# One pass instead of two for the second half's operands, and stores and loads two at a time, in the FFN of a one-core encoder block

## The chip, the cores and the metric

The kernel runs on one core of a Trainium2 chip. The metric is the device time of one execution in microseconds (us); lower is better. The time before is the median of three runs.

## What is computed

The kernel computes one layer of an encoder for 2048 tokens of width 1024: three gated token mixers, then a feed-forward network with a causal convolution of width 3, then a last norm. The change touches only the feed-forward part and the last norm:

```python
def conv_ffn(h, w_in, conv_w, conv_b, w_out):
    u, gv = jnp.split(h @ w_in, 2, axis=-1)
    T = u.shape[1]
    up = jnp.pad(u, ((0, 0), (CONV_W - 1, 0), (0, 0)))
    uc = conv_w[0] * up[:, 0:T]
    for j in range(1, CONV_W):
        uc = uc + conv_w[j] * up[:, j:j + T]
    uc = uc + conv_b
    return (jax.nn.gelu(uc, approximate=False) * gv) @ w_out
...
        x = x + conv_ffn(rms_norm(x, norm_ffn_g[l]), w_ffn_in[l], ffn_conv_w[l],
                         ffn_conv_b[l], w_ffn_out[l])
    return rms_norm(x, norm_final_g)
```

D_FF is 2816, so `w_ffn_in` is 1024 by 5632 and `w_ffn_out` 2816 by 1024. Everything is float32; each float32 product is made of three matmuls on a high and a low part (hi*hi, hi*lo, lo*hi).

## The kernel before

Tokens lie on the free axis, channels on the 128 partitions. The feed-forward part (`ffn`) works on two halves of 1024 tokens (`hf` 0 and 1), each of two tiles of 512 tokens (`t` 0 and 1). The 2816 inner channels are 22 blocks `f` of 128.

**First product.** `in_block(f)` makes the 128 channels of u and of the gate for both token tiles with seven products instead of eight (a Strassen-like scheme). Each product is 12 matmuls of 128x128 by 128x512 and needs one weight piece `wsp` of 512 KB, and for each a right operand `B[m][k]`, m from 1 to 7 and k from 0 to 3, 128x512 in hi and lo. The order of the products is 1, 2, 6, 5, 3, 7, 4. In the second half the weight pieces are read from a cache in DRAM (`wc_w_ffn_in`).

**The operands.** `ffn_prep(hf, B)` makes them from `x2d` (the residual stream in DRAM). `quarter(k, t)` loads a block of 128 channels by 512 tokens (256 KB) into one of eight staging places and norms it with one VectorE (DVE) instruction, a scalar_tensor_tensor on line 725 (L725). `put` writes a block as hi (a copy on ScalarE, ACT, L729) and lo (a subtract on DVE, L730); `minus` is a subtract on DVE (L733). Block pair k has the four quarters b11, b12, b22 and b21. B[1] and B[2] are b11 and b21 as they are and lie in the tile `hA`; the other five are differences. A first loop norms b11 and b21 of each k and puts them into `hA`; a second loop norms all four quarters of each k (so b11 and b21 again) and makes the other five. The generator gives way eight times, four per loop.

**Second product.** `out_group(f0)` multiplies two blocks f with `w_ffn_out`: 16 output tiles (8 channel blocks d by 2 token tiles), each 6 matmuls into a PSUM bank (L924 to L926) and one DVE add into the accumulator `acc` in SBUF (L928). Its weights are four pieces per group (`w_out`), each loaded as 256 KB into `wraw`, cast to hi on ACT (L138) and subtracted to lo on GpSimd (POOL, L141). `wraw` has three buffers, and staging places of `quarter` are `wraw` buffers too.

**Where the halves meet.** At the end of the first half stand two groups, `out_group(NF - 4)` (banks `mx` and `ch`) and `out_group(NF - 2)` (banks `mm`), 32 tiles in all. After every third tile (`SK = 3`) `step()` takes one step of `ffn_prep(1)`. These groups I call A and B.

**The start of the second half.** During f = 0 and 1 the first half's `acc` is squared and summed; `finish_scale` (L802 on DVE, L800 on POOL) then scales its 16 tiles. Each is stored to `out` (256 KB), and when its store has landed the same buffer takes the residual for the second half (`acc<-x2d`, 256 KB). These 16 stores and 16 loads stand in a list `turns` of 20 entries: entry n holds store n (n < 16) and load n - 4 (n >= 4). `hook` takes three entries from the list after each of the products 3 to 6 of f = 2 and after each product of f = 3. Between the third and the fourth product of f = 3 comes `out_group(0)`, called through `mid`.

All these transfers, and the weights, are issued by SyncE (SP) in one order; an SP instruction that waits holds back all that stand behind it. The order on each engine is set when the program is built: a scheduler places the instructions, and `tc.issue_after(ins)` ties an instruction's place to that of another.

Of the kernel before, what the change touches and what calls it, by code (L numbers as in the profile page):

```python
# [22 lines left out]
TT = 512  # L23
# [58 lines left out]
def block_kernel(ctx: ExitStack, tc, A, out, T=2048):  # L82
    nc = tc.nc
    NT = T // TT
    te, ve, sc, gp = nc.tensor, nc.vector, nc.scalar, nc.gpsimd

    def dma(o, i):
        nc.sync.dma_start(o, i)
# [19 lines left out]
    def bank(tag, bufs=1):  # L108
        return ps.tile([P, 512], F32, tag=tag, name=tag, bufs=bufs)
# [116 lines left out]
    def bcast(dst, src):  # L226
        dma(dst, src.rearrange("(o t) -> o t", o=1).to_broadcast([P, src.shape[0]]))
# [39 lines left out]
    def cc(name, b):  # L267
        return col[:, ROFF[name] + b:ROFF[name] + b + 1]
# [439 lines left out]
    def ffn_prep(hf, B):  # L708

        rsb = [keepf["s1"], keepf["12"]]  # L710
        for t in range(2):
            bcast(rsb[t], rs2d[hf * 1024 + t * TT:hf * 1024 + t * TT + TT])

        staged = [0]

        def quarter(k, t):

            place = ("wraw", "raw", "22", "wraw", "11", "raw", "wraw", "21")[staged[0] % 8]
            staged[0] += 1
            if place in keepf:  # L720
                b = keepf[place]
            else:
                b = sb.tile([P, TT + 2 * (place == "raw")], F32, tag=place, name="stage", bufs=3 if place == "wraw" else 2)[:, 0:TT]
            dma(b, x2d[k, :, hf * 1024 + t * TT:hf * 1024 + t * TT + TT])
            ve.scalar_tensor_tensor(b, b, cc("norm_ffn_g", k), rsb[t], ALU.mult, ALU.mult)  # L725
            return b

        def put(o, src):
            sc.copy(o[:, 0], src)  # L729
            ve.tensor_tensor(o[:, 1], src, o[:, 0].bitcast(F32), ALU.subtract)  # L730

        def minus(dst, a, b):
            ve.tensor_tensor(dst, a, b, ALU.subtract)  # L733

        def blocks(t):
            return [t[:, :, k, :] for k in range(4)]

        hA = sb.tile([P, 2, 2, 4, TT], F32R, tag="hA", name="hA")
        B[1], B[2] = blocks(hA[:, 0]), blocks(hA[:, 1])
        for k in range(4):  # L740
            put(B[1][k], quarter(k, 0))
            put(B[2][k], quarter(4 + k, 0))
            yield
        for m, tag in ((6, "g16"), (5, "z16"), (3, "macc"), (7, "ya")):
            B[m] = blocks(sb.tile([P, 2, 4, TT], F32R, tag=tag, name=f"B{m}"))
        B[4] = [sb.tile([P, 2, TT], F32R, tag=t, name="B4", bufs=2) for t in ("LP", "LP", "BKt", "BKt")]
        for k in range(4):
            b11, b12, b22, b21 = quarter(k, 0), quarter(k, 1), quarter(4 + k, 1), quarter(4 + k, 0)
            minus(b11, b12, b11)
            put(B[5][k], b11)  # L750
            minus(b12, b22, b12)
            put(B[3][k], b22)
            minus(b11, b22, b11)
            put(B[6][k], b11)
            put(B[7][k], b12)
            minus(b21, b11, b21)
            put(B[4][k], b21)
            yield

    def acc_view(acc, d, tk):  # L760
        t = tk.start // TT
        return acc[d][t][:, tk.start - t * TT:tk.stop - t * TT]
# [46 lines left out]
    def ffn(prep):  # L809
# [10 lines left out]
        B = prep  # L820
        ahead = {}
        for hf in range(T // 1024):
# [88 lines left out]
            def w_out(f, n):  # L911
                return split_piece(A["w_ffn_out"][f * P:(f + 1) * P, n * 512:(n + 1) * 512], 512, True)[1:]

            def out_tile(G, ws, d, tk, tag):
                n = tk.stop - tk.start
                t = tk.start // TT
                tt = slice(tk.start - t * TT, tk.stop - t * TT)
                if tag == "ch":
                    turn[0] ^= 1
                    tag = ("ch", "mx")[turn[0]]  # L920
                a = bank(tag, 4 if tag == "mm" else 2)[:, :n]
                cs = slice(d % 4 * P, (d % 4 + 1) * P)
                for j in range(2):
                    te.matmul(a, ws[j][0][:, cs], G[j][t][:, 0, tt], start=j == 0, stop=False)  # L924
                    te.matmul(a, ws[j][0][:, cs], G[j][t][:, 1, tt], start=False, stop=False)  # L925
                    te.matmul(a, ws[j][1][:, cs], G[j][t][:, 0, tt], start=False, stop=j == 1)  # L926
                ac = acc_view(acc, d, tk)
                ve.tensor_tensor(ac, ac, a, ALU.add)  # L928

            tiles, turn = [0], [0]  # L930

            def step():

                tiles[0] += 1
                if steps is not None and tiles[0] % SK == 0:
                    next(steps, None)

            def out_group(f0, G, last):
                if not last:
                    if f0 < NF - 4:  # L940
                        for n in range(2):
                            ws = [w_out(f0 + j, n) for j in range(2)]
                            for d in range(4 * n, 4 * n + 4):
                                for t in range(2):
                                    out_tile(G, ws, d, slice(t * TT, t * TT + TT), "ch")
                        return
                    ws = [[w_out(f0 + j, n) for j in range(2)] for n in range(2)]
                    for t in range(2):
                        for d in range(8):
                            out_tile(G, ws[d // 4], d, slice(t * TT, t * TT + TT), "ch")  # L950
                            step()
                    return
# [7 lines left out]
                ws = [[w_out(f0 + j, n) for j in range(2)] for n in range(2)]  # L960
# [38 lines left out]
            turns = []  # L999

            def hook():

                for _ in range(3):
                    if turns:
                        turns.pop(0)()

# [2 lines left out]
            for f in range(NF):  # L1009
# [14 lines left out]
                G = LazyTiles(lambda t: sb.tile([P, 2, TT], F32R, tag=tags[t], name="G"))  # L1024
# [32 lines left out]
            if hf + 1 < T // 1024:  # L1057
                prep = {}
                steps = ffn_prep(hf + 1, prep)
# [4 lines left out]
            B = prep  # L1064
# [11 lines left out]
    for i in range(NT):  # L1076
# [109 lines left out]
        for tok in ORDER:  # L1186
            k, n = tok[0], int(tok[1:] or 0)
            a = at["a"]
# [45 lines left out]
        if i + 1 < NT:  # L1234
            mgb, mga = (sb.tile([P, 2, 4, TT], F32R, tag=t, name="mg") for t in ("z16", "g16"))
            mgs = [(mga if d >= 4 else mgb)[:, :, d % 4, :] for d in range(8)]
            steps = None
        else:
            mgs = [sb.tile([P, 2, TT], F32R, tag=t, name="mg", bufs=2 if t == "x" else 1)
                   for t in ("TBa", "TBb", "kT", "vM", "BK", "UV", "SV", "x")]  # L1240
            ffn_tiles()
            steps = ffn_prep(0, prep)
# [26 lines left out]
        ssums[i] = ssum  # L1269

    ffn(prep)


# [66 lines left out]
```

## Time and profile before

| what | us |
|---|---|
| median of 3 runs (lowest, highest) | 3349.37 (3346.64, 3349.82) |
| profiled execution, own time | 3354.97 |
| its span, first to last instruction | 3353.1 |
| granted TensorE clock, mean over the span | 0.974 |

The span is what the views divide; the profiled execution's own time is 1.9 us longer. Times of views are counted from the span's start.

### The profile page before, as it was taken

Reading aid. Unit: us, or ns where it says so; the run is one execution under the profiler, and the core shown is the slowest. Engines: PE = TensorE matmul, PEld = TensorE weight load, DVE = VectorE, ACT = ScalarE, POOL = GpSimd, SP = SyncE. Lnnn points to the kernel's source line nnn. Section 1 sums busy time; section 2 is a strip of 40 time slices with the busy share of each in tenths; the row PEclk is TensorE's granted clock in tenths of the full one; section 3 lists DMA queues with packets and bytes.
Section 4 is the critical chain, followed back from the end, with each engine's and each line's share of the span. In section 5 each row is a group of like instructions: output and inputs, shape, how many; then the busy total and the mean of one; then the engine's idle time right before and its main releaser. Section 6 shows DMA issues by size and latency. Waiting matters only on the chain. (4 is left out here: it accounts for less than half of the span.)

```text
span 3353.1 us, 44925 instructions
## 1 busy us (share of the span) xinstructions
PE 3141.3 (94%) x16224; PEld 2482.3 (74%) x16224; DVE 2149.9 (64%) x4022; ACT 1127.7 (34%) x2063; POOL 940.4 (28%) x1096
## 2 busy tenths in 40 slices
PE   6878898999999999999999999999999889999998
PEld 5656676766777777786777778888887668888887
DVE  4887732787544887338875766666668655555556
ACT  4545442444223343324332433333233411121213
POOL 2354443122101122011222055445453121010103
PEclk9999998999999999999999999999999999999999
DMA  7455577445574454663454865445455464443442
GB/s 246 151 175 193 190 234 248 129 141 154 166 237 151 128 160 144 204 204 123 131 167 157 267 238 187 163 180 178 163 189 168 140 201 138 151 138 130 147 146 90
DMA packets 237518, 573.82 MB, mean 171 GB/s; under 512 B 58224, under 2 KB 70128, under 8 KB 237168
## 3 DMA queue, kind: packets, MB, share of 16 engines
q1 hardware_dynamic: 237296, 570.95, 51.6%
q8 instruction: 129, 2.11, 0.3%
q14 instruction: 93, 0.76, 0.1%
HBM read 408.30 MB, written 162.54 MB: 170 GB/s over the span
## 5 line engine op out<-in xcount | busy, mean ns | idle before, releaser
L172 PE MATMUL mm<-h,wsp 128*128 128x512 f32 x4032 | 1100.8, 412 | 8.9 <-ACT wsp L138 3.5
L172 PEld LDWEIGHTS mm<-h,wsp 128*128 128x128 f32 x4032 | 736.5, 192 | 164.2 <-issue 10.0
L141 POOL TENSOR_TENSOR wsp<-wraw,wsp 128x512 fp32r<-128x512 f32 x196 | 270.4, 1384 | 368.3 <-ACT wsp L138 290.6
L858 PE MATMUL mm<-B,wsp 128*128 128x512 f32 x880 | 347.9, 395 | 6.9 <-DMA wsp<-wc_w_ffn_in 4.1
L860 PE MATMUL mm<-B,wsp 128*128 128x512 f32 x880 | 347.4, 395 | 1.9 <-POOL wsp L845 1.9
L859 PE MATMUL mm<-B,wsp 128*128 128x512 f32 x880 | 345.7, 393 | 0.0
L591 DVE TENSOR_TENSOR XX<-XX,As 128x16 f32<-128x16 f32 (+30 forms) x496 | 232.9, 470 | 8.9
L656 POOL TENSOR_SCALAR SV<-SV,dC 64x64 f32<-64x64 f32 x224 | 116.5, 520 | 384.7 <-DVE SV L667 261.6
L172 PE MATMUL mm<-mg,wsp 128*128 128x512 f32 x768 | 187.7, 405 | 20.2 <-ACT wsp L138 8.3
L858 PEld LDWEIGHTS mm<-B,wsp 128*128 128x128 f32 x880 | 166.1, 189 | 44.5 <-DVE U L902 2.5
L860 PEld LDWEIGHTS mm<-B,wsp 128*128 128x128 f32 x880 | 166.0, 189 | 41.5 <-POOL wsp L845 2.9
L859 PEld LDWEIGHTS mm<-B,wsp 128*128 128x128 f32 x880 | 166.0, 189 | 37.9
L172 PEld LDWEIGHTS mm<-mg,wsp 128*128 128x128 f32 x768 | 148.4, 195 | 59.3 <-ACT wsp L138 9.6
L871 ACT ACTIVATE tg<-U,cwu 128x512 f32<-128x512 f32 x88 | 71.8, 816 | 336.0 <-DVE U L902 276.1
L138 ACT CAST wsp<-wraw 128x512 fp32r<-128x512 f32 x204 | 125.3, 618 | 174.6 <-PE mm L172 40.7
L928 DVE TENSOR_TENSOR acc<-acc,mx 128x512 f32<-128x512 f32 x160 | 109.8, 686 | 87.6 <-PE mx L926 87.1
L882 POOL COPY cwu<-U 128x2 f32<-128x2 f32 x88 | 40.4, 459 | 411.3 <-DVE U L902 271.9
L593 DVE TENSOR_REDUCE XX<-XX 128x8 f32<-128x16 f32 (+30 forms) x496 | 144.2, 291 | 9.4
L928 DVE TENSOR_TENSOR acc<-acc,ch 128x512 f32<-128x512 f32 x140 | 96.0, 686 | 83.2 <-PE ch L926 83.2
L858 PE MATMUL mm<-hA,wsp 128*128 128x512 f32 x352 | 139.0, 395 | 8.1 <-DMA wsp<-wc_w_ffn_in 6.5
L860 PE MATMUL mm<-hA,wsp 128*128 128x512 f32 x352 | 139.0, 395 | 0.4 <-POOL wsp L845 0.4
L859 PE MATMUL mm<-hA,wsp 128*128 128x512 f32 x352 | 138.8, 394 | 0.0
(389 smaller groups left out, 5998.0 us busy)
## 6 DMA issues: line engine op xcount, KB each, us to landing
wc_w_ffn_in<-wsp SPq DMA_DIRECT2D x154, 512.0 KB, 2.9
wsp<-wc_w_ffn_in SPq DMA_DIRECT2D x154, 512.0 KB, 3.5
wsp<-wc_w_gate SPq DMA_DIRECT2D x144, 512.0 KB, 3.5
wsp<-wc_w_in_mix SPq DMA_DIRECT2D x108, 512.0 KB, 3.3
wc_w_gate<-wsp SPq DMA_DIRECT2D x48, 512.0 KB, 2.9
wsp<-wc_w_o SPq DMA_DIRECT2D x48, 512.0 KB, 5.1
wraw<-in_w_ffn_out SPq DMA_DIRECT2D x88, 256.0 KB, 2.7
wc_w_in_mix<-wsp SPq DMA_DIRECT2D x36, 512.0 KB, 2.9
```

Source lines behind the costliest of these rows:

```text
L138: sc.copy(hi, raw[:, :n])
L141: (ve if early[0] >= 0 else gp).tensor_tensor(lo, raw[:, :n], hi.bitcast(F32), ALU.subtract)
L172: mm = te.matmul(*args, **kw)
L591: ve.tensor_tensor(xm[:, :, 0:t + 1], X[:, :, 0:t + 1], As[:, 0:t + 1, t].unsqueeze(1).to_broadcast([P, 8, t + 1]), ALU.mult)
L593: ve.tensor_reduce(X[:, :, t:t + 1], xm[:, :, 0:t + 1], AX.X, ALU.add)
L656: gp.tensor_scalar(SV[hs, hh, c + 1, :], SV[hs, hh, c, :], dC[hs, c + 1:c + 2], None, ALU.mult)
L858: te.matmul(acc, w[:, 0, ks], B[m][k][:, 0], start=k == 0, stop=False)
L859: te.matmul(acc, w[:, 0, ks], B[m][k][:, 1], start=False, stop=False)
L860: mm = te.matmul(acc, w[:, 1, ks], B[m][k][:, 0], start=False, stop=k == 3)
L871: sc.activation(uc, U[:, 2:TT + 2], AF.Identity, bias=cw[:, 66 + f:67 + f], scale=cw[:, 44 + f:45 + f])
L882: gp.tensor_copy(ucar[:, f, :], U[:, TT:TT + 2])
L928: ve.tensor_tensor(ac, ac, a, ALU.add)
```

## The change

In the second half the first loop of `ffn_prep` is left out. Its two puts move into the one loop that is left, which gives way twice for each k, so eight times as before. `hook` takes two entries from `turns` instead of three. What is then left in the list when `out_group(0)` comes is taken one entry after each output tile.

```diff
         B[1], B[2] = blocks(hA[:, 0]), blocks(hA[:, 1])
-        for k in range(4):
+        for k in range(4 if hf == 0 else 0):
             put(B[1][k], quarter(k, 0))
             put(B[2][k], quarter(4 + k, 0))
             yield
...
         for k in range(4):
-            b11, b12, b22, b21 = quarter(k, 0), quarter(k, 1), quarter(4 + k, 1), quarter(4 + k, 0)
+            if hf == 0:
+                b11, b12, b22, b21 = quarter(k, 0), quarter(k, 1), quarter(4 + k, 1), quarter(4 + k, 0)
+            else:
+                b11, b12 = quarter(k, 0), quarter(k, 1)
+                put(B[1][k], b11)
+                b22, b21 = quarter(4 + k, 1), quarter(4 + k, 0)
+                put(B[2][k], b21)
+                yield
             minus(b11, b12, b11)
...
-                    te.matmul(a, ws[j][1][:, cs], G[j][t][:, 0, tt], start=False, stop=j == 1)
+                    mm = te.matmul(a, ws[j][1][:, cs], G[j][t][:, 0, tt], start=False, stop=j == 1)
                 ac = acc_view(acc, d, tk)
                 ve.tensor_tensor(ac, ac, a, ALU.add)
+                return mm
...
-                                    out_tile(G, ws, d, slice(t * TT, t * TT + TT), "ch")
+                                    mm = out_tile(G, ws, d, slice(t * TT, t * TT + TT), "ch")
+                                    if turns:
+                                        with tc.issue_after(mm.ins):
+                                            turns.pop(0)()
...
-                for _ in range(3):
+                for _ in range(2):
                     if turns:
                         turns.pop(0)()
```

How the rows stand on two engines. In the changed program L935 is the add that was L928.

DVE, between groups A and B, before: the first rows are the end of the second loop's k = 1 (`B4` from `a21`), and the adds are those of group B (`mm`).

```order
L928 TENSOR_TENSOR acc_16955<-acc_16955,mm_21775 128x512
L730 TENSOR_TENSOR B4_21671<-a21_16024,B4_21671 128x512
L928 TENSOR_TENSOR acc_16959<-acc_16959,mm_21783 128x512
L725 SCALAR_TENSOR_TENSOR stage_21791<-stage_21791,par_83,x1_16021 128x512
L725 SCALAR_TENSOR_TENSOR stage_21794<-stage_21794,par_83,a12_16023 128x512
L725 SCALAR_TENSOR_TENSOR tw_16022<-tw_16022,par_83,a12_16023 128x512
```

DVE at the same work of the change (k = 1 ends, k = 2 begins):

```order
L935 TENSOR_TENSOR acc_16965<-acc_16965,ch_21678 128x512
L935 TENSOR_TENSOR acc_16969<-acc_16969,mx_21686 128x512
L730 TENSOR_TENSOR B4_21538<-a21_16024,B4_21538 128x512
L725 SCALAR_TENSOR_TENSOR stage_21694<-stage_21694,par_83,x1_16021 128x512
L725 SCALAR_TENSOR_TENSOR stage_21697<-stage_21697,par_83,a12_16023 128x512
L725 SCALAR_TENSOR_TENSOR tw_16022<-tw_16022,par_83,a12_16023 128x512
L730 TENSOR_TENSOR hA_21532<-stage_21694,hA_21532 128x512
```

The end of k = 1 now falls within group A (15 adds stand ahead of it instead of 16 of A and 4 of B), and the puts into `hA` stand in the middle of the work of each k.

SP, the four weight pieces of group B (`wraw`) among the loads of staged quarters, before:

```order
L88 DMA stage_21682<-x2d_60 128x512
L88 DMA stage_21745<-x2d_60 128x512
L88 DMA wraw_21707<-in_w_ffn_out 128x512
L88 DMA wraw_21712<-in_w_ffn_out 128x512
L88 DMA wraw_21717<-in_w_ffn_out 128x512
L88 DMA tw_16022<-x2d_60 128x512
L88 DMA stage_21794<-x2d_60 128x512
L88 DMA wraw_21722<-in_w_ffn_out 128x512
```

SP at the same place of the change:

```order
L88 DMA stage_21704<-x2d_60 128x512
L88 DMA wraw_21717<-in_w_ffn_out 128x512
L88 DMA stage_21793<-x2d_60 128x512
L88 DMA tw_16022<-x2d_60 128x512
L88 DMA wraw_21722<-in_w_ffn_out 128x512
L88 DMA a21_16024<-x2d_60 128x512
L88 DMA wraw_21727<-in_w_ffn_out 128x512
L88 DMA wraw_21732<-in_w_ffn_out 128x512
L88 DMA stage_21798<-x2d_60 128x512
```

Before, the first piece stands behind 15 of the 24 staged quarters and the last behind 17; now the first stands behind 12 of 16 and the last behind 15.

SP in f = 2 and 3 of the second half, from one weight piece of the first product to the next, before:

```order
L88 DMA wsp_22442<-wc_w_ffn_in_16614 128x1024
L88 DMA out<-acc_16961 128x512
L88 DMA acc_22458<-x2d_60 128x512
L88 DMA out<-acc_16963 128x512
L88 DMA acc_22461<-x2d_60 128x512
L88 DMA out<-acc_16965 128x512
L88 DMA acc_22464<-x2d_60 128x512
L88 DMA wsp_22471<-wc_w_ffn_in_16614 128x1024
```

and of the change:

```order
L88 DMA wsp_22438<-wc_w_ffn_in_16614 128x1024
L88 DMA out<-acc_16959 128x512
L88 DMA acc_22454<-x2d_60 128x512
L88 DMA out<-acc_16961 128x512
L88 DMA acc_22457<-x2d_60 128x512
L88 DMA wsp_22461<-wc_w_ffn_in_16614 128x1024
```

Between two weight pieces there are four transfers of 256 KB instead of six. Ahead of the piece of the third product of f = 3 stand 14 stores and 10 loads instead of 16 and 14; the other eight transfers now come behind it, with the weights of `out_group(0)` among and behind them.

## Rows read from the trace of the kernel before

**Rows 1.** The page, section 4: the chain that ended last, by engine.

```profile
PE 35%; DVE 2%; DMA 2%; POOL 1%; issue 1%; ACT 0%; SPq 0%; POOLq 0%; DVEq 0%; ACTq 0%
```

**Rows 2.** Windows: length, busy us (x instructions) by engine, clock, DMA share, GB/s.

```profile
2480.00:2560.00 80.00, 79.98 (x349) 65.08 (x348) 55.69 (x71) 28.48 (x46) 38.66 (x36) 1.00 0.58 201
2560.00:2634.00 74.00, 55.66 (x204) 40.93 (x202) 69.57 (x109) 26.78 (x44) 11.85 (x9) 0.91 0.39 114
...
2690.00:2728.00 38.00, 26.12 (x96) 19.66 (x95) 18.18 (x21) 6.04 (x9) 10.30 (x12) 0.91 0.96 303
2728.00:2752.00 24.00, 24.00 (x105) 19.36 (x104) 11.13 (x17) 2.18 (x4) 3.93 (x4) 1.00 0.25 84
```

**Rows 3.** Waits of PE from 2560 to 2634 us: total, times, longest.

```profile
PE mm L924 <- DVE acc L928: 12.4, 6, 3.6
```

**Rows 4.** Timeline of DVE: start, duration, line, out and in.

```profile
2559.25 0.81 DVE L725 SCALAR_TENSOR_TENSOR a<-a,par,x 128x512 f32<-128x512 f32 x1 [2.27 <-DMA a<-x2d]
...
2609.36 0.68 DVE L730 TENSOR_TENSOR B<-a,B 128x512 fp32r<-128x512 f32 x1
...
2622.41 0.74 DVE L725 SCALAR_TENSOR_TENSOR a<-a,par,x 128x512 f32<-128x512 f32 x1
2623.08 0.68 DVE L733 TENSOR_TENSOR tw<-stage,tw 128x512 f32<-128x512 f32 x1
2623.68 0.68 DVE L730 TENSOR_TENSOR B<-stage,B 128x512 fp32r<-128x512 f32 x1
...
2629.09 0.68 DVE L730 TENSOR_TENSOR B<-a,B 128x512 fp32r<-128x512 f32 x1
2629.69 2.47 DVE L928 TENSOR_TENSOR acc<-acc,mm 128x512 f32<-128x512 f32 x4
...
2633.97 0.69 DVE L928 TENSOR_TENSOR x<-x,mm 128x512 f32<-128x512 f32 x1 [0.67 <-PE mm L926]
```

**Rows 5.** The chain that ended last, from 2583 us: start, us, what.

```profile
2583.27 2.63 DMA wraw<-in_w_ffn_out
2586.00 0.63 ACT wsp L138
2586.70 1.49 POOL wsp L141
2588.21 2.72 DMA wraw<-in_w_ffn_out
...
2597.72 4.83 DMA stage<-x2d
```

**Rows 6.** DMA from 2690 to 2728 us: sum, then issues, KB each, us to landing.

```profile
DMA packets 5492, 11.52 MB, mean 303 GB/s; under 512 B 608, under 2 KB 608, under 8 KB 5491
...
out<-acc SPq DMA_DIRECT2D x13, 256.0 KB, 7.4
wsp<-wc_w_ffn_in SPq DMA_DIRECT2D x5, 512.0 KB, 7.3
```

**Rows 7.** Timeline of PE: starts of products after a wait.

```profile
2701.62 0.70 PE L858 MATMUL mm<-B,wsp 128*128 128x512 f32 x1 [2.10 <-DMA wsp<-wc_w_ffn_in]
...
2707.75 0.47 PE L858 MATMUL mm<-B,wsp 128*128 128x512 f32 x1 [1.55 <-DVE sx L906]
...
2715.20 0.64 PE L858 MATMUL mm<-hA,wsp 128*128 128x512 f32 x1 [4.44 <-DMA wsp<-wc_w_ffn_in]
2715.63 0.63 PE L859 MATMUL mm<-hA,wsp 128*128 128x512 f32 x1
...
2721.51 0.47 PE L858 MATMUL mm<-hA,wsp 128*128 128x512 f32 x1 [1.73 <-DMA wsp<-wc_w_ffn_in]
...
2726.79 0.47 PE L858 MATMUL mm<-B,wsp 128*128 128x512 f32 x1 [2.05 <-DMA wsp<-wc_w_ffn_in]
```

**Rows 8.** Timeline of SP: issues, with the time to the last of a group.

```profile
2690.03 3.66 SPq L88 DMA_DIRECT2D out<-acc  x3
...
2695.27 0.43 SPq L88 DMA_DIRECT2D wsp<-wc_w_ffn_in  x1
```

## The prediction, made before the run

> **What bounds the kernel now.** I read the chain that ended last first: it runs mainly through PE [rows 1], so the question is where PE stands still near the edit. A table of windows answers it. In the 80 us before the halves meet PE is busy throughout at full clock, one matmul every 0.229 us [rows 2]. Then come two bad stretches. From 2560 to 2634 us (groups A and B) PE is busy 55.7 of 74 us and starts 204 matmuls, which at 0.229 us would take 46.7 us: 27 us are lost. From 2690 to 2728 us (f = 2 and 3 of the second half) it starts 96, worth 22.0 us, in 38 us: 16 us are lost. In `out_group(0)` behind it nothing is lost (105 matmuls in 24 us) and the DMA share is only 0.25 [rows 2].
>
> The two stretches have different limits. In the first DVE is busy 69.6 of 74 us [rows 2], and the waits of PE name its adds: 12.4 us in the `mm` banks alone [rows 3]. DVE is the bound: PE's tiles wait for banks that DVE empties late, since operand work stands between the adds. In the second the DMA engines are full (share 0.96, 303 GB/s) [rows 2, 6], and PE waits at the start of five products in a row, 2.10 + 1.55 + 4.44 + 1.73 + 2.05 = 11.9 us [rows 7]. The second of these waits is put down to DVE, but that instruction is one that PE needed earlier; the weight piece is the likelier releaser, since the four around it are weight pieces. The queue explains it: a weight piece is issued behind stores and loads of accumulators, which take 7.4 us to land when the engines are full [rows 6].
>
> **The single pass.** It takes away 8 loads of 256 KB and 8 DVE instructions on L725. Neighbours in DVE's timeline start 0.66 us apart on L725 and 0.60 on L730 and L733 [rows 4]. So 8 x 0.66 = 5.3 us of DVE time go, from a stretch where DVE is the bound. Puts, subtracts, casts and adds keep their number.
>
> The order on the engine says where the rest goes. From the L725 at 2559.25 to the last `B4` (start 2629.09) DVE has 103 rows before and 95 now. Before, 23 of them are L725: 23 x 0.66 + 80 x 0.60 = 63.2 us against 69.8 to the last one's start [rows 4]; some 7 us are waits and long rows. Now the end of k = 1 stands 54 rows behind that L725 (7 of them L725): 32.8 us, plus about 2 for the long rows of the conv that I leave in, so it falls at 2594.1 instead of 2610.0 [rows 4]. There are 41 rows left (8 L725), 25.1 us, so DVE alone would end at 2619.2 instead of 2629.7: 10.5 us sooner. That is the upper bound.
>
> Against it stands the wait that comes next. All four weight pieces of group B go, one after the other, through one `wraw` buffer, and each takes 4.94 us from issue to issue (load, cast on ACT, subtract on POOL) [rows 5]. Before, they began at 2583.27, and the last staged quarter behind them came with the chain [rows 5]. Now the first piece stands behind b22 of k = 1, whose buffer comes free seven rows ahead of the end of k = 1: 2594.1 - 7 x 0.60 is about 2590. The fourth piece is then whole at 2590 + 4 x 4.94 = 2610. The fifth add of group B needs a tile made with it, and DVE stands there some 2 to 4 us. Behind that add stand 20 rows to the last `B4`, 4 of them L725: 12.2 us. With 1.2 us for the tile and the add itself this makes 2623.5 instead of 2629.7: **6 us** sooner. Behind the last `B4` six adds are left in either order, and PE needs the same 4 us or so to its last tile [rows 4]. Queued behind the waiting add is the work for k = 3, which only the second half's first products wait for; queued behind SP's waits are only that half's first weights, with 20 us to spare. If the chain slips by one piece, 5 us of the 6 are gone. So 1 to 10.5, and I take 6.
>
> The puts into `hA` of k = 3 now come at the end instead of the beginning; they stand ahead of the last `B4`, so the first product, which needs them, waits for nothing new. Had they no cover, they would cost two rows, 1.2 us.
>
> **Two at a time.** Nothing is removed: 32 transfers of 256 KB stay. Between two weight pieces there are now four instead of six, and eight, two stores and six loads, come behind the piece for the third product of f = 3. At 303 GB/s 256 KB take 0.87 us and a weight piece 1.73 [rows 6]. Pieces came 6.3 us apart on average before: 2701.62 to 2726.79 for four [rows 7], which is 6 x 0.87 + 1.73 = 6.9 by the rate, so it is DMA that set them. Now four transfers and a piece are 5.2 us by the rate, and 4.8 if they too come a little faster than it. I take 5.0.
>
> Step by step: the piece of the sixth product of f = 2 was issued behind six stores and two loads at 2695.27; now it stands behind four stores, of which the last are ready at about 2692, as three issues took from 2690.03 to 2693.7 [rows 8]. It lands before PE is through with the fifth product at 2699.5 (2701.62 less the wait of 2.10) [rows 7], and that wait goes. A product is 12 x 0.229 = 2.75 us. The seventh piece comes at about 2701, in time; those of f = 3 at 2706, 2711 and 2716. PE ends its second product of f = 3 at 2713.9. Before the third the order now has ten matmuls of `out_group(0)` on its first piece, 2.3 us, which fill the gap; the third product runs from 2716.2 to 2719 instead of 2726.79 to 2729.5. Then PE waits for the second piece of `out_group(0)`, which stands four transfers behind: 5 x 0.87 = 4.3 us after 2716, plus some 2 us for cast and subtract (0.63 and 1.3 to 1.5) [rows 5]: 2722.4. There 3 us are given back. Of the 96 matmuls some 82 are left, 18.8 us: the end is at 2741 to 2742, instead of 2752 [rows 2]. The last two pieces stand behind eight more transfers, 7 us: about 2729, when tile 8 wants them; I take off 1 us. That makes **9 us**. The eight late transfers are covered by the idle DMA of this stretch (share 0.25, 84 GB/s; 2.1 MB more in 24 us are 87 GB/s) [rows 2]; without it they would cost their 7 us there. Each late load is wanted several tiles after it lands. Bounds: six transfers fewer ahead of the third product, 5.2 us, less the 2 for the piece: 3; all five waits gone: 12.
>
> The clock needs a word. After a wait matmuls start 0.43 us apart for a while (2715.20 to 2715.63) [rows 7] instead of 0.229, PE having stood for 4.44 us. In my sum that is worth nothing, for a product at the low level, 12 x 0.43 = 5.2 us, was still done before the next weights came. The Trainium skill (TensorE: Matmul & The Clock Gate, HAM oscillation) says that a wait for DMA sends the clock to half and that half of the slow time is then lost; the row agrees that it falls. A mean clock of 0.91 over the stretch's 38 us [rows 2] is 6.8 us at the low level; by that rule half of it, 3.4 us as an estimate, would come on top of my sum.
>
> **The sum.** 6 + 9 = 15 us from the profiled execution's own 3354.97 makes 3340. That execution is 5.6 us above the median of the runs, 3349.37, so the runs should show **3334**.
>
> **The rivals.**
> - *Only the stores and loads pay* (3340). The weight chain of group B begins 5 us or more later than I reckon, and DVE's freed time is spent waiting at that fifth add. For it: the chain does begin later than before (2583.27). Against it: DVE's work ahead of it shrank by more.
> - *Only the pass pays* (3343). The bytes are the same, and PE meets in `out_group(0)` the time that it saved in f = 3. The Trainium skill (DMA: Bandwidth & Descriptors, Issuing engines are not separate DMA queues) has all queues share the same DMA engines, so that order alone makes no bandwidth. For it: share 0.96 now; against it: 0.25 right behind [rows 2].
> - *Neither* (3349): both wait again at the next link, the pieces of group B and of group 0.
> - *Slower* (3374). The six late turns go one by one, since each load waits for its buffer's store to land and SP holds back all behind it. Six landings of 7.3 us [rows 6] instead of 7 us in all put the last pieces of `out_group(0)` off from 2729 to about 2766, some 37 to 40 us; less 15, that is 25 slower. It decides from 2.5 us more per turn on. Against it: 303 GB/s times 7.3 us are 2.2 MB, eight transfers in flight at once [rows 6], and each store stands four turns ahead of the load that reuses its buffer.
>
> **How the numbers follow.** Forecast 0.60, only stores and loads 0.15, only the pass 0.08, neither 0.10, slower 0.07. Changes within 0.2%, 6.7 us, cannot be told from none here. The forecast is faster but for its lowest corner (0.58), the stores alone mostly (0.13), the pass alone in half of its cases (0.04): faster 0.75, same 0.18, slower 0.07. The range takes in both bounds, 22 us faster (3327) to 4 us (3345), and one us for the spread of runs: 3327 to 3346.
>
> **What would show it.** L725 in the stretch from 2559 on has 8 instances fewer; the last `B4` comes about 6 us sooner; PE's waits for DVE in group B shrink, and a wait for the fourth `wraw` piece stands ahead of its fifth tile. In f = 2 and 3 the weights come about 5 us apart, the waits of the sixth and seventh product are gone, and PE waits a few us at the second piece of `out_group(0)`. Wrong would be: group B ends as late as before with DVE idle; `out_group(0)` with long waits for its last pieces or for late accumulators; or the second half's first product waiting for `hA`.

## The result and the profile after

The change is faster. Its median is 3329.05 us (3328.03 to 3335.68, 4 runs) where the kernel before has 3348.76 (3346.64 to 3349.82, 4 runs) beside it: a ratio of 0.9947 [0.9936, 0.9959]. Timed twice more in later sets (e0 and e12 below) it gave 0.9948 [0.9934, 0.9962] and 0.9937 [0.9923, 0.9951]. The forecast was 3334 (3327 to 3346).

In the changed program L858 to L860 are L865 to L867, L885 is L892, L906 is L913, L924 to L926 are L931 to L933, L928 is L935. The profiled execution took 3328.50 us, its span 3326.5.

**The chain that ended last** (page, section 4; compare [rows 1]) has the same shares by engine as before: a gain of half a per cent of the span does not show at this grain, and the stretches have to be looked at.

```profile
PE 35%; DVE 2%; DMA 2%; POOL 1%; issue 1%; ACT 0%; SPq 0%; POOLq 0%; ACTq 0%; DVEq 0%
```

**Windows**, with the columns of [rows 2]. The first is where the halves meet, the second f = 2 and 3 with the beginning of `out_group(0)`, the third the rest of that group.

```profile
2560.00:2634.00 74.00, 61.70 (x231) 45.88 (x232) 60.15 (x94) 23.74 (x39) 8.66 (x9) 0.91 0.37 120
...
2690.00:2728.00 38.00, 34.29 (x145) 26.48 (x144) 16.28 (x24) 5.03 (x8) 5.62 (x7) 1.00 0.74 252
2728.00:2752.00 24.00, 24.00 (x106) 19.53 (x105) 14.14 (x19) 6.85 (x11) 6.79 (x8) 1.00 0.38 128
```

In the same windows PE starts 231 matmuls instead of 204, and 145 instead of 96; the clock of the second is 1.00 instead of 0.91. Part of this is that everything comes some 10 us earlier, so each stretch is looked at from its own marks below.

**Where the halves meet: waits of PE** (total, times, longest; compare [rows 3]) and **DVE's timeline** (compare [rows 4]).

```profile
PE mm L931 <- ACT wsp L138: 6.9, 4, 4.0
PE mx L931 <- DVE acc L935: 3.2, 1, 3.2
PE mm L933 <- POOL wsp L141: 2.4, 3, 1.3
PE mm L931 <- DVE acc L935: 1.5, 2, 1.3
```

```profile
2549.47 0.75 DVE L725 SCALAR_TENSOR_TENSOR a<-a,par,x 128x512 f32<-128x512 f32 x1 [2.42 <-DMA a<-x2d]
...
2583.76 0.70 DVE L730 TENSOR_TENSOR B<-a,B 128x512 fp32r<-128x512 f32 x1
2584.36 1.77 DVE L725 SCALAR_TENSOR_TENSOR stage<-stage,par,x 128x512 f32<-128x512 f32 x1
...
2589.85 0.68 DVE L730 TENSOR_TENSOR hA<-stage,hA 128x512 fp32r<-128x512 f32 x1
2592.24 1.28 DVE L935 TENSOR_TENSOR acc<-acc,mm 128x512 f32<-128x512 f32 x2 [1.71 <-PE mm L933]
...
2595.25 1.77 DVE L733 TENSOR_TENSOR stage<-tw,stage 128x512 f32<-128x512 f32 x1
...
2600.48 1.35 DVE L730 TENSOR_TENSOR B<-stage,B 128x512 fp32r<-128x512 f32 x1 [1.05 <-ACT B L729]
...
2614.61 0.69 DVE L730 TENSOR_TENSOR B<-a,B 128x512 fp32r<-128x512 f32 x1
...
2619.18 0.69 DVE L935 TENSOR_TENSOR x<-x,mm 128x512 f32<-128x512 f32 x1 [0.67 <-PE mm L933]
```

PE's 12.4 us of waits in the `mm` banks for DVE are down to 1.5; in their place stand 6.9 and 2.4 us for the weight pieces (1.3 and 1.3 before). From the first L725 shown to the last `B4` DVE needs 65.1 us instead of 69.8. It waits for PE once (1.71 us) and has three rows that are longer than usual (1.77, 1.77 and 1.35 us). The pieces themselves, SP's issues and POOL's subtracts (compare [rows 5]):

```profile
2580.32 0.33 SPq L88 DMA_DIRECT2D wraw<-in_w_ffn_out  x1
2585.62 0.33 SPq L88 DMA_DIRECT2D wraw<-in_w_ffn_out  x1
...
2583.91 1.68 POOL L141 TENSOR_TENSOR wsp<-wraw,wsp 128x512 fp32r<-128x512 f32 x1 [23.23 <-ACT wsp L138]
2589.29 2.36 POOL L141 TENSOR_TENSOR wsp<-wraw,wsp 128x512 fp32r<-128x512 f32 x1 [3.70 <-ACT wsp L138]
2594.95 1.52 POOL L141 TENSOR_TENSOR wsp<-wraw,wsp 128x512 fp32r<-128x512 f32 x1 [3.30 <-ACT wsp L138]
...
2600.01 1.28 POOL L141 TENSOR_TENSOR wsp<-wraw,wsp 128x512 fp32r<-128x512 f32 x1 [1.74 <-ACT wsp L138]
```

**Two at a time: PE's starts after waits** (compare [rows 7]) and **SP's issues around the second piece of `out_group(0)`** (compare [rows 8]).

```profile
2687.24 0.47 PE L865 MATMUL mm<-B,wsp 128*128 128x512 f32 x1 [1.22 <-DMA wsp<-wc_w_ffn_in]
2692.32 0.47 PE L865 MATMUL mm<-hA,wsp 128*128 128x512 f32 x1 [2.05 <-DVE tg L892]
2696.08 0.47 PE L865 MATMUL mm<-hA,wsp 128*128 128x512 f32 x1 [0.74 <-DMA wsp<-wc_w_ffn_in]
2705.34 0.50 PE L931 MATMUL mx<-G,wsp 128*128 128x512 f32 x1 [0.41 <-ACT wsp L138]
2706.69 0.50 PE L933 MATMUL mx<-G,wsp 128*128 128x512 f32 x1 [0.39 <-POOL wsp L141]
```

```profile
2697.54 0.70 SPq L88 DMA_DIRECT2D wraw<-in_w_ffn_out  x1
2698.28 0.56 SPq L88 DMA_DIRECT2D out<-acc  x1
2699.38 0.32 SPq L88 DMA_DIRECT2D acc<-x2d  x1
2701.39 0.34 SPq L88 DMA_DIRECT2D out<-x  x1
2701.99 3.60 SPq L88 DMA_DIRECT2D acc<-x2d  x4
2706.51 0.32 SPq L88 DMA_DIRECT2D x<-x2d  x1
2706.88 1.38 SPq L88 DMA_DIRECT2D wraw<-in_w_ffn_out  x3
```

Of the 11.9 us of waits 4.0 are left ahead of the third product of f = 3, and 0.8 at the second piece of `out_group(0)`. The wait that names `tg` is one for weights too: the piece of that product landed at 2692.18 us, 0.14 us ahead of PE's start. (In the trace of before the same holds for the wait that names L906 [rows 7]: its piece landed at 2707.62 us.) The last eight transfers, two stores and six loads behind the second piece, go out within 8.6 us, although loads and stores take 6.4 and 6.9 us to land in the median of this stretch (DMA issues of 2675 to 2713 us; compare [rows 6]):

```profile
acc<-x2d SPq DMA_DIRECT2D x15, 256.0 KB, 6.4
out<-acc SPq DMA_DIRECT2D x12, 256.0 KB, 6.9
```

### The profile page after: what moved, and what is told of

Its sections match the earlier page's. It is cut to its first block, busy times and chain, and to the rows that moved or that the text cites. A ratio compares the mean times of both kernels' runs of the same rounds, so it can differ in the third digit from the quotient of the medians.

```text
span 3326.5 us, 44899 instructions
## 1 busy us (share of the span) xinstructions
PE 3129.4 (94%) x16224; PEld 2476.1 (74%) x16224; DVE 2143.7 (64%) x4014; ACT 1128.0 (34%) x2063; POOL 941.1 (28%) x1096
## 5 line engine op out<-in xcount | busy, mean ns | idle before, releaser
L865 PE MATMUL mm<-B,wsp 128*128 128x512 f32 x880 | 346.8, 394 | 1.3 <-DMA wsp<-wc_w_ffn_in 1.2
L867 PE MATMUL mm<-B,wsp 128*128 128x512 f32 x880 | 346.3, 393 | 1.7 <-POOL wsp L852 1.7
L867 PEld LDWEIGHTS mm<-B,wsp 128*128 128x128 f32 x880 | 165.2, 188 | 41.0 <-POOL wsp L852 2.7
L865 PEld LDWEIGHTS mm<-B,wsp 128*128 128x128 f32 x880 | 165.4, 188 | 37.9 <-DVE tg L880 1.6
L935 DVE TENSOR_TENSOR acc<-acc,mx 128x512 f32<-128x512 f32 x160 | 110.0, 687 | 87.2 <-PE mx L933 86.7
L935 DVE TENSOR_TENSOR acc<-acc,ch 128x512 f32<-128x512 f32 x140 | 96.2, 687 | 81.1 <-PE ch L933 80.3
L865 PE MATMUL mm<-hA,wsp 128*128 128x512 f32 x352 | 138.9, 395 | 4.8 <-DVE tg L892 2.1
L867 PE MATMUL mm<-hA,wsp 128*128 128x512 f32 x352 | 139.1, 395 | 0.5 <-POOL wsp L852 0.4
```

What stands on the lines that cost most here:

```text
L865: te.matmul(acc, w[:, 0, ks], B[m][k][:, 0], start=k == 0, stop=False)
L867: mm = te.matmul(acc, w[:, 1, ks], B[m][k][:, 0], start=False, stop=k == 3)
```

## Marks that make the traces comparable

Executions of one program differ ahead of everything that the change touches. As a mark I take the last eight matmuls of the residual's statistics (`mx<-one,ssum`), which come early in the first half; their row starts at 1971.38 us in the trace of before and at 1962.03 in that of after, and over all traces, whose work ahead of it is the same, between 1960.3 and 1971.6. So of the 26.6 us between the two spans 9.4 are none of the change. The table counts from the mark to the last add of group B, and from there to the end of the span. It adds how many matmuls PE started in two stretches behind that add: from 20 to 56 us (f = 0 and 1 of the second half) with the granted clock, and from 56 to 94 us (f = 2 and 3). The runs e0 to e12 are those of the next section.

| kernel | mark to last add of B | last add to end | f = 0, 1: matmuls (clock) | f = 2, 3: matmuls |
|---|---|---|---|---|
| before | 662.6 | 719.1 | 152 (0.86) | 96 |
| the change | 657.2 | 707.3 | 158 (0.91) | 138 |
| the change, e0 | 657.7 | 708.5 | 148 (0.82) | 142 |
| the change, e12 | 656.0 | 705.8 | 163 (0.95) | 141 |
| e1 | 656.7 | 716.1 | 156 (0.91) | 103 |
| e2 | 662.6 | 708.8 | 152 (0.86) | 143 |
| e3 | 660.8 | 719.0 | 147 (0.82) | 101 |
| e4 | 659.3 | 713.6 | 161 (0.95) | 108 |
| e5 | 658.0 | 704.0 | 158 (0.91) | 153 |
| e7 | 653.8 | 710.4 | 147 (0.82) | 140 |
| e9 | 658.1 | 708.6 | 152 (0.86) | 134 |
| e10 | 656.6 | 705.6 | 163 (0.95) | 143 |
| e11 | 655.8 | 706.6 | 151 (0.86) | 155 |

The third column of the same program varies by 2.7 us. It goes with the clock in f = 0 and 1, which the kernels do not touch: 15 matmuls between 0.82 and 0.95, at 0.229 us each [rows 2] 3.4 us. In the second column e1, e4 and e5 run the change's code; with its own three traces that makes six, from 656.0 to 659.3. A difference within these 3 us says nothing there.

## The experiments

The first set ran on one chip, where the kernel before took 3350.05 us (33 runs). Diffs are against the change where nothing else is said.

**e1_pass_only.** The single pass alone; the list of transfers as before.

```diff
-                                    if turns:
-                                        with tc.issue_after(mm.ins):
-                                            turns.pop(0)()
...
-                for _ in range(2):
+                for _ in range(3):
```

> The single pass alone, stores and loads three at a time as before. Theory (two separate gains: 8 DVE instructions of 0.66 us where DVE is the bound, and eight transfers moved behind a weight piece where DMA is full): 5 to 6 us faster than before, and the waits at the starts of the products of f = 2 and 3 stay at some 12 us. Rival (the stores and loads bring all, DVE's freed time is spent waiting for the weight pieces of group B): within 2 us of before.

Measured: 3344.67 us, ratio 0.9984 [0.9975, 0.9993], so 5.4 us by the medians; the last add of group B comes 5.9 us sooner after the mark. In f = 2 and 3 PE still waits 8.8 us for weights. The pass pays, on its own, what it pays in the change.

**e2_spread_only.** The two loops as before; the list two at a time and among the tiles.

```diff
-        for k in range(4 if hf == 0 else 0):
+        for k in range(4):
...
-            if hf == 0:
+            if True:
```

> Stores and loads two at a time alone, both loops of the operand pass as before. Theory: 9 to 12 us faster than before, so that this and the pass alone add up to the whole gain of the change (some 17 to 20 us). Rival (the bytes are the same, PE meets the time again in the output group behind): within 3 us of before.

Measured: 3340.04 us, 0.9974 [0.9965, 0.9983], 10.0 us by the medians. Group B ends as before (662.6 from the mark), and all of the gain, 10.3 us, lies behind it. The gains of e1 and e2 add up to 15.4 us by medians and 19.3 from the mark, the change's own were 16 to 21 by medians in three sets and 15.5 to 19.9 from the mark: two separate gains, no sign that they help or hinder each other; the interval of each is some 3 us either way.

**e3_loads_kept.** The eight multiplies of the second half's first loop are left out, its loads and puts stay. Against the kernel before:

```diff
-        def quarter(k, t):
+        def quarter(k, t, norm=True):
...
-            ve.scalar_tensor_tensor(b, b, cc("norm_ffn_g", k), rsb[t], ALU.mult, ALU.mult)
+            if norm:
+                ve.scalar_tensor_tensor(b, b, cc("norm_ffn_g", k), rsb[t], ALU.mult, ALU.mult)
...
-            put(B[1][k], quarter(k, 0))
-            put(B[2][k], quarter(4 + k, 0))
+            put(B[1][k], quarter(k, 0, hf == 0))
+            put(B[2][k], quarter(4 + k, 0, hf == 0))
```

> The kernel before, with the eight norm multiplies of the first loop left out in the second half; their eight loads and all puts stay (that part of the operands is then not normed). Theory (DVE instructions are what the pass saves): about 5 us faster than before, as the pass alone. Rival (the loads and the staging buffers that they hold are what it saves): within 1 us of before.

Measured: 3346.22 us, 0.9989 [0.998, 0.9998], 3.8 us by the medians; group B's end 1.8 us sooner after the mark. Between the first add of group A and the last of B the eight multiplies did give 4.4 us (63.7 us before, 59.2 here), but the first add came 2.6 us later after the mark (601.5 instead of 598.9), with DVE waiting 2.0 us for a copy into `hA` ahead of it. Between these two adds the multiplies give nearly what the whole pass gives there (4.5 to 6.2 us in six traces). What put off the first add is not settled; that loads and place of the first loop have a price of their own is not shown, since 3.8 and 5.4 us by the medians lie within each other's intervals.

**e4_flush.** What is left of the list goes out at once, ahead of the weights of `out_group(0)`.

```diff
                     if f0 < NF - 4:
+                        while turns:
+                            turns.pop(0)()
...
-                                    if turns:
-                                        with tc.issue_after(mm.ins):
-                                            turns.pop(0)()
```

> The change, but what is left of the stores and loads when the output group comes is issued at once ahead of it, instead of one entry after each tile. Theory (what counts is the eight transfers behind the weight piece of the third product of f = 3): most of the gain stays, 2 to 4 us slower than the change because the second to fourth weight pieces of the output group stand behind all eight transfers (7 us). Rival (it is the taking one by one among the tiles that pays): 8 us or more slower than the change, as the pass alone.

Measured: 3343.4 us, 0.9979 [0.997, 0.9987]: more of the gain is lost than the 2 to 4 us that I had expected. By the medians 6.7 us are left, 1.3 more than the pass alone gave; against the change's ratios of 0.9937 to 0.9948 it is 10 to 14 us slower, which is what the rival said. Behind group B the end is 5 to 8 us later than in the three traces of the change, and one wait names it:

```profile
PE mx L931 <- ACT wsp L138: 7.2, 1, 7.2
```

PE stands for 7.2 us at `out_group(0)`, whose second piece is now issued behind eight transfers. So two per product are not the whole gain: the places among the tiles are half of it or more by this trace (behind group B 5.5 us are left, of 10.3 in e2 and 10.6 to 13.3 in the change), and nearly all of it by the medians.

The second set: the kernel before 3350.9 us (9 runs).

**e0_after.** The change, unedited.

> The change itself, timed beside the three below. If pass and spread are two separate gains: the single pass alone was worth 5.4 us and the spread alone 10.0 us in the first set, so the change should be 13 to 18 us below the kernel before (ratio 0.9947 to 0.9961). If the two help each other (leftover turns that find a freer queue because the operands end sooner, or the reverse), it is 20 us or more below.

Measured: 3334.95 us, 0.9948 [0.9934, 0.9962], 16.0 us below before. In the range of two separate gains.

**e5_one.** One entry per product.

```diff
-                for _ in range(2):
+                for _ in range(1):
```

> The change with one entry of the list per product instead of two, so that 13 instead of 8 transfers of each kind come among the tiles of out_group(0). Theory (DMA sets the pace of f = 2 and 3; in out_group(0) it has room): the weights of f = 2 and 3 come sooner still; but PE's waits there are down to 4.4 us in the change's trace, so at most 4 us faster than the change. Rival (the late loads are what limits from here on: the accumulators of the tiles that have just begun are loaded only a tile or two ahead of the adds that want them, and the weight pieces of out_group(0) stand behind them): 2 to 8 us slower than the change, with DVE's adds or PE waiting for acc or for wraw pieces in out_group(0).

Measured: 3330.66 us, 0.994 [0.9927, 0.9952]. In f = 2 and 3 PE starts 153 matmuls instead of 138 to 142 and waits for no weight of the first product. What it waits for from 2670 to 2730 us:

```profile
PE mx L931 <- ACT wsp L138: 1.2, 1, 1.2
PE mx L933 <- POOL wsp L141: 0.9, 2, 0.6
PE mx L223 <- POOL rs L213: 0.7, 1, 0.7
```

The late accumulators cost nothing to speak of: one add of the group waited for its load, 0.70 us, beside PE's next tile. Eleven to fifteen matmuls more are some 3 us; the medians' 4.3 us below e0 agree, but the intervals of the two overlap.

**e9_hA_pool.** The low parts of B[1] and B[2] by POOL.

```diff
-        def put(o, src):
+        def put(o, src, eng=ve):
             sc.copy(o[:, 0], src)
-            ve.tensor_tensor(o[:, 1], src, o[:, 0].bitcast(F32), ALU.subtract)
+            eng.tensor_tensor(o[:, 1], src, o[:, 0].bitcast(F32), ALU.subtract)
...
-                put(B[1][k], b11)
+                put(B[1][k], b11, gp)
...
-                put(B[2][k], b21)
+                put(B[2][k], b21, gp)
```

> The change with the eight subtracts that make the low part of B[1] and B[2] of the second half on POOL instead of DVE. Theory that DVE is still what sets the end of group B: eight rows of 0.60 us less on DVE, so 2 to 5 us faster than the change. Rival (group B of the change is set by its weight pieces, one buffer, 5.4 us per piece, each with a subtract on POOL): no gain, 0 to 1 us; and if POOL's subtracts of some 1.3 us come ahead of those of the pieces, 1 to 4 us slower.

Measured: 3334.26 us, 0.9949 [0.9936, 0.9961]; group B ends 658.1 us after the mark. No gain, though DVE has eight rows of 0.60 us less, but not for the reason that the rival gives. DVE's other rows grew longer: all twelve that take over 1 us in this stretch begin while a POOL subtract runs. Two pairs of its timeline and POOL's:

```profile
2594.37 1.75 POOL L730 TENSOR_TENSOR hA<-stage,hA 128x512 fp32r<-128x512 f32 x1 [1.27 <-ACT hA L729]
...
2598.20 1.74 POOL L730 TENSOR_TENSOR hA<-stage,hA 128x512 fp32r<-128x512 f32 x1
```

```profile
2594.89 1.78 DVE L725 SCALAR_TENSOR_TENSOR stage<-stage,par,x 128x512 f32<-128x512 f32 x1
...
2598.71 1.78 DVE L730 TENSOR_TENSOR B<-tw,B 128x512 fp32r<-128x512 f32 x1
```

An L725 takes 1.78 us instead of 0.75, an L730 1.78 instead of 0.68. From the L725 ahead of group A (2555.95 us) to the end of the last `B4` DVE is busy 63.1 us for 88 rows; in the three traces of the change it is 61.8, 63.5 and 63.7 us for 95. The mean row takes 0.72 us instead of 0.65 to 0.67, and DVE's busy time does not fall.

**e7_no_lo.** The pieces of group B get no low part; the third matmul of each product reads the high part again.

```diff
+            if not lo_too:
+                return w, hi, hi
             (ve if early[0] >= 0 else gp).tensor_tensor(lo, raw[:, :n], hi.bitcast(F32), ALU.subtract)
...
-                ws = [[w_out(f0 + j, n) for j in range(2)] for n in range(2)]
+                ws = [[w_out(f0 + j, n, hf > 0) for j in range(2)] for n in range(2)]
```

> The change, but the weight pieces of the first half's group B get no low part: the subtract on POOL is left out and the third matmul of each product reads the high part again (so the lo*hi part of that group is left out; PE's matmuls, DVE's adds and all loads stay). A piece's round from issue to issue should shrink from about 5.4 to about 3.7 us. Theory (the chain of the four pieces sets when group B's late tiles start): 2 to 5 us faster than the change, with the last add of group B that much sooner. Rival (DVE's rows set it, the chain is met just in time): within 1 us of the change, apart from up to 1.3 us by DVE rows that no longer run beside POOL's subtracts.

Measured: 3327.05 us, 0.9931 [0.9919, 0.9944]. The pieces come 3.6 us apart (issues at 2580.06, 2583.60, 2587.19), and group B ends 653.8 us after the mark, 3.1 us sooner than the mean of the change's three traces (656.9). That is what the theory of the chain asked for. But two things changed at once: the chain is shorter, and POOL no longer works beside DVE. In this trace DVE has no row above 0.9 us between 2557 us and the end of group B, while the trace of after has three, worth (1.77 - 0.75) + (1.77 - 0.68) + (1.35 - 0.68) = 2.8 us. So e7 does not tell the two apart; e10 shortens the chain alone. By the medians it is 7.9 us below e0, but the intervals of the two overlap, and from the mark to the end its trace takes 1364.2 us where those of the change take 1361.8 to 1366.2.

The third set: the kernel before 3347.01 us (11 runs).

**e10_places.** Other staging places for k = 2 and 3, so that the four pieces have three `wraw` buffers. (Its L933, L935 and L937 are L931, L933 and L935 of the change.)

```diff
             place = ("wraw", "raw", "22", "wraw", "11", "raw", "wraw", "21")[staged[0] % 8]
+            if hf > 0 and staged[0] >= 8:
+                place = ("22", "raw", "11", "raw", "21", "wraw", "wraw", "22")[staged[0] - 8]
```

> The change with other staging places for k = 2 and 3 of the second half's operands: the quarters of k = 2 go into the places 22, raw, 11, raw, those of k = 3 into 21, wraw, wraw, 22; nothing of the computation is left out. So when group B's four weight pieces are allocated no wraw buffer holds a quarter of k = 2, and the pieces have three buffers instead of one. Theory (the pieces' chain through one buffer sets the end of group B; without their low part its last add came 3.5 us sooner): the pieces are issued within a few us of each other, PE's 7 us of waits for ACT and 2 us for POOL in group B go, and the last add comes 2 to 5 us sooner than in the change. Rival (the chain is met by DVE's rows, and the 3.5 us came from POOL's subtracts that no longer slow DVE): 0 to 1 us, with PE waiting for DVE's adds in place of the casts.

Measured: 3331.03 us, 0.9948 [0.9935, 0.9961]; e12, the change beside it, 3325.75. The four pieces are issued within 8.8 us, and PE's waits for them are gone. What PE waits for instead from 2540 to 2640 us, and the busy times from 2559 to 2616 us (windows; the third pair is DVE's):

```profile
PE mm L933 <- DVE acc L937: 11.8, 5, 7.1
PE mx L933 <- DVE acc L937: 3.6, 1, 3.6
```

```profile
2559.00:2616.00 57.00, 42.03 (x160) 31.57 (x158) 55.89 (x88) 22.01 (x37) 12.13 (x7) 0.91 0.29 93
```

DVE is busy 55.9 of 57 us, and group B ends 656.6 us after the mark, within the change's own 656.0 to 657.7. From the first add of group A to the last of B it takes 56.9 us (e11 with the same places 57.0), where the six traces with the change's order take 57.5 to 59.1: in the mean the chain may be worth 1.5 us, not the 2 to 5 us of my theory. What sets the end is DVE's rows, with the length that some of them have beside POOL's.

**e11_places_one.** e10 and one entry per product (`range(1)` as in e5).

> The places of the run above and one entry of the list per product instead of two. One entry alone took 4.3 us off the change's median (3.8 us between the last add of group B and the end). If the two gains are separate: 6 to 9 us faster than the change, about 3326 to 3329 us where the change has 3335. If the weights of the second half's first products, issued behind the staged quarters, become the next wait: no faster than the one-entry run alone, with PE waiting for wsp at f = 0.

Measured: 3330.08 us, 0.9948 [0.9936, 0.9961]. In f = 2 and 3 PE starts 155 matmuls (153 in e5) and waits for no weights of the first product; from the mark to the end 1362.4 us as in e5 (1362.0), where the change has 1361.8 to 1366.2. By the medians it is not faster than the change beside it.

**e12_after_again.** The change, unedited.

> The change again, for the comparison with the two runs above: 14 to 20 us below the kernel before.

Measured: 3325.75 us, 0.9937 [0.9923, 0.9951], 21.3 us below before. The best traces of one entry per product show some 3 us more in f = 2 and 3 than the change, but no run time here separates e5 or e11 from it: e5 lies 4.3 us below e0, e11 4.3 us above e12. That stays open.

## Why the prediction was right, and where its steps were not

**The single pass** was put at 6 us sooner for the end of group B; measured were 5.4, 4.9 and 6.6 in the change and 5.9, 3.3 and 4.6 in e1, e4 and e5, 5.1 in the mean. The size is about right, the step behind it is not. The prediction had DVE alone end 10.5 us sooner and gave 4.5 of it back to a chain of weight pieces. Its places came out to the microsecond: the end of k = 1 34.9 us behind the first L725 (34.8 forecast), the first piece issued 30.9 us behind it (30.8 forecast), the fourth whole at 51.8 (50.8 forecast). But DVE does not stand at the fifth add of group B: it waits 1.71 us for PE at the first one, and in the traces of e0 and e12 for PE only ahead of the last, 0.67 us, as in all traces. The bound of 10.5 was mis-sized: it left in 2 of the 7 us of waits and long rows of before, without a reason why the rest should go. They stayed: from the first L725 to the end of the last `B4` the change takes 65.7 us, 7.8 more than the 57.9 of its rows at 0.66 and 0.60 us, and before it was 70.4, 7.2 more than 63.2. In the trace of after DVE idles 4.0 of these 65.7 us, in e0 1.9 of 65.3 and in e12 1.1 of 64.9, where longer rows take the place of the waits. What remains is what was removed, eight rows of 0.66 us, 5.3 us. So 6 came out by luck: a bound 5 us too high, less 4.5 us for a chain that, taken away (e10), gives 1.5 us at most.

**PE's waits changed their name.** 9.3 us of waits for casts and subtracts of pieces stand in the trace of after, and e10 turned them into 11.8 us of waits for DVE with nearly the same end. The releaser that comes last for PE is not the bound as long as another is due just behind it.

**Two at a time** was put at 9 us. Three traces with the old list (before, e1, e3) start 96, 103 and 101 matmuls in f = 2 and 3, the three of the change 138, 142 and 141: 40 more, at 0.229 us 9.2 us. Two of its steps were off, and in opposite ways. PE was to wait 3 us for the second piece of `out_group(0)`: it waits 0.8, for that piece came out at 2697.5 us and was cast 7.1 us later, just as PE came to it. And three waits were to be gone that are only shorter, 1.22, 2.05 and 0.74 us. The wait of tile 8 (1 us) did not come, or with 0.29 us at most (e12). So the forecast had some 3 us of waits too many in `out_group(0)` and 4.0 us too few at the products, and that the sum still came out at 9 is luck as well. The count of transfers was off too. In the trace the piece of the third product of f = 3 is issued at 2693.45 us, behind 12 stores and 8 loads, not 14 and 10 as said above; those stand ahead of the second piece of `out_group(0)`. In the trace of before 16 and 14 stand ahead of the third product's piece. So it is ten transfers fewer, not six; at the forecast's 0.87 us each they are 8.7 us, and the lower bound of 3 us was reckoned too low. The sum step by step counts the four transfers between the two pieces and does not change by this.

**The clock.** In this stretch it is 1.00, 0.99 and 0.96 in the three traces of the change, counted from the last add of group B, instead of 0.91. The prediction held that the low clock costs nothing of its own in a sum that goes by the arrival of weights, and that sum came out. Counted by waits it is seen again: 11.9 us of them shrank to 4.8 in the trace of after, 7.1 us, and the rest is the clock: 6.8 us at the low level, one matmul per 0.43 us [rows 7], are 16 matmuls where 30 would have been started, 14 of 0.229 us or 3.2 us. Together 10.3. The Trainium skill (TensorE: Matmul & The Clock Gate, HAM oscillation) has half of the time at the low clock lost, and by these rows that holds (3.2 of 6.8 us). It is another way to count the same time and must not be put on top of a sum by arrivals. Not every wait brings the low clock: in the trace of after it stays at 1.00 through waits of 1.22, 2.05 and 0.74 us.

**The rest.** From the mark the change is 17.2, 15.5 and 19.9 us shorter than before, against a forecast of 15. What is above the two terms follows the clock of f = 0 and 1, 11 matmuls more (2.5 us) in e12 and 4 fewer (0.9 us) in e0: scatter, not the change. That the trace of before stood some 5 us above its median was allowed for.

**The rivals.** Only the stores and loads, or only the pass: e1 and e2 each show the other half. Neither: no. Slower, by late turns that wait for each other's landings: it needed 2.5 us per turn; the last loads go out about 1 us apart (2701.99 us to 2706.51 for five), and even with 13 turns among the tiles (e5) no wait of PE for them shows. The order did make time without making bandwidth: DMA is as full in f = 2 and 3 as before (a share of 0.91 to 0.96 there), and what was moved fell into the idle engines behind.

## What to carry to other kernels

When transfers that nobody needs yet stand between weights in one queue, move them to where the DMA share is low, one by one among the tiles; put in a block there, they move the wait (e4: half of the gain lost or more). Where two releasers come due close together, take one away alone before you believe the one that the waits name: here the weight pieces were named, and without them DVE set nearly the same time. And count rows in a stretch that begins at a mark inside the kernel; executions of the same code differ by 11 us ahead of it.

## What the hardware showed beyond that

A DVE row of two operands in SBUF that begins while a POOL subtract runs is held up: those above take 1.35 to 1.78 us instead of 0.68 or 0.75. It goes the other way too: the POOL subtract at 2589.29 us began just behind a DVE row, another DVE row of 0.68 us followed without a gap, and the subtract took 2.36 us where the last one took 1.28. So eight subtracts given to POOL (e9) took eight rows of 0.60 us off DVE, and its busy time stayed. The Trainium skill (SBUF — State Buffer, Who interferes with whom) says that a DVE instruction with two SBUF inputs contends with a GpSimd instruction that reads SBUF, and the one that comes second is held up; the long L725, L730 and L733 rows above all have two such inputs and begin while POOL's row runs, and the long POOL row began behind DVE's, so the traces agree.

The clock of f = 0 and 1 of the second half differs between executions of the same code: in 13 traces it is 0.82, 0.86, 0.91 or 0.95 over 36 us, with PE busy 33.2 to 33.8 us in all of them. In windows of the change, of e0 and of e12:

```profile
2639.18:2675.18 36.00, 33.76 (x158) 28.01 (x157) 24.82 (x33) 17.97 (x30) 19.09 (x17) 0.91 0.35 119
```

```profile
2647.10:2683.10 36.00, 33.74 (x148) 28.24 (x147) 23.12 (x32) 18.03 (x30) 17.42 (x16) 0.82 0.31 103
```

```profile
2637.56:2673.56 36.00, 33.25 (x163) 27.71 (x162) 25.62 (x34) 17.83 (x30) 20.08 (x17) 0.95 0.38 130
```

The matmuls follow it: 158, 148 and 163. What decides it in an execution no run here shows.
